# Gate projections and the first heads' keys and queries by Strassen's seven products, in a first stage of their own

## The chip, the core and the metric

The kernel runs on one core of one Trainium2 chip. The metric is the device time of one execution in microseconds (us). The engines are named as the profile names them: PE is the tensor engine with its products and transposes, DVE the vector engine, ACT the scalar engine, POOL the engine that masks and that issues the accumulating transfers, SP the engine that issues the other transfers.

## What is computed

One decoder layer for 1024 tokens with 1024 channels. All data is float32.

```
h = rmsnorm(x, norm1_g) * (1 + sc1) + sh1
p = h @ w_in                                   # 1024 x 7168
xr, yr, q, k, v, ga, gb = split(p, 7)          # components 0 to 6, 8 heads of 128 each
y_a = rg_lru(causal_dwconv(xr)) * gelu(yr)
y_b = stick_breaking_attention(rmsnorm(q), rmsnorm(k), v)
mix = sigmoid(ga) * y_a + sigmoid(gb) * y_b
x = x + gt1 * (mix @ w_out)
h2 = rmsnorm(x, norm2_g) * (1 + sc2) + sh2
g, v = split(causal_dwconv(h2 @ ffn_up), 2)
x = x + gt2 * ((gelu(g) * v) @ ffn_down)
```

sc, sh and gt are slices of c @ ada_w + ada_b, the modulation, computed on DVE as dot products. Stick-breaking attention weighs key j for query i by beta_ij times the product of (1 − beta) over the keys between them; DVE forms that product with a scan.

## The kernel before

Every factor of a product is split into a high part, rounded to the format PE takes, and a low part, the rest. A product then is three PE passes: high by high, high by low, low by high. The high part is an ACT copy or activation; the low part is a DVE subtraction (lo_of). So a projection of one component and head, 1024 inputs to 128 outputs for 1024 tokens, is 8 blocks x 3 passes x 2 halves of the tokens = 48 products of 128x512 (gemm, L150).

The program's stages, in order:

- The first stage is ordered by hand (manual_schedule). It loads the eight token tiles xr, squares all of them on ACT (L218), takes one reciprocal root on DVE, norms the tiles (L231 on DVE, L229 on ACT), and then goes through units of a channel block j and a half of the tokens hf: four transposes on PE (px, L238), two activations that modulate (hh, the high part, and hn), the low part on DVE (hl). The projections of k, q and the second branch's gate of head 0 (components 3, 2, 6, listed in FIRST) follow unit by unit in six banks of PSUM. The modulation of a channel block is two dot products over 1024 elements on DVE (L135) with two small operations (scale_shift); it stands between the units, two channel blocks ahead.
- Then eight attention heads. Here a scheduler orders the instructions by priority; with high_priority code goes ahead of what was written before it. For head h: qk(h) projects keys and queries, takes statistics st on PE, a root on DVE, sends the root through DRAM (rkd, rb), and makes the keys kh, kl. values(h), for two heads at a time, projects v. attention(h) goes through four groups of two query blocks: scores z (L418 to L420), two sigmoids on ACT, masks on POOL, the scan on DVE (L436), a multiply on DVE (L440), transposes tp on PE (L444), high and low parts ah, al, and the weighted sum py (L457). Each group also does one dot product of the modulation for later stages. gate_b(h) projects the gate of the second branch (component 6), and its sigmoid stays in the tiles sg until the head's output is multiplied.
- After head 7, early_ga projects the first branch's gate (component 5) of heads 0 to 3 into tiles of their own. The scheduler spreads these products over attention(7).
- The RG-LRU stage (lru_head, gate(1, h), lru_tail) goes over eight heads and projects the gate of component 5 for heads 4 to 7. Then out_block, the output projection.
- The FFN's up-projection runs by Strassen's seven products: the two rows of outputs (columns f and f + 24), the two halves of the inputs and the two halves of the tokens are a 2x2 by 2x2 block product, done with 7 half-size products instead of 8. A half-size product is 4 blocks x 3 passes = 12 products of 128x512. Sums of weight blocks are made by transfers that accumulate in SBUF (POOL issues them, L764); sums of h are made on DVE. For the first six columns, products 1 and 2 run early, with the first half of the tokens, and their results go to DRAM (yed).

Each engine executes its instructions in program order; an instruction that waits holds back all behind it on its engine.

## Time and profile before

| | |
|---|---|
| median of 3 runs | 1669.05 us (1667.24 to 1669.6) |
| profiled execution | 1669.8 us, of which the span of the profile is 1668.1 |
| mean granted clock of PE | 0.999 |
| 0 to 71 us | first stage |
| 71 to 645 us | attention heads |
| 645 to 852 us | RG-LRU stage |
| 852 to 983 us | output projection and the FFN's start |
| 983 to 1402 us | FFN, up |
| 1402 to 1668 us | FFN, down |

The limits of the stages are read from the timeline to about 10 us; they overlap. In the views, a row of groups reads: line, engine, operation, output <- inputs, shapes, count | busy time in all, mean ns of one | idle time before them and what ended it. A row of the timeline reads: start, duration, engine, line, operation, count, and in brackets how long the engine had waited and for what.

### The profile page before, as it was taken

To read this page: it belongs to the slowest core of one execution; us is meant where nothing else is said; L and a number is where in the kernel's file an instruction comes from. 1 tells how busy PE (TensorE), PEld (TensorE's weight loads), DVE (VectorE), ACT (ScalarE), POOL (GpSimd) and SP (SyncE) were. 2 spreads that over 40 slices of the span, in tenths; PEclk is the share of its full clock that TensorE was granted. 3 is DMA by queue.
4 is the path that set the end of the run, shared out by engine and by line. 5 is a ranking of instruction groups with operands and counts; after the bars stand their busy time and mean duration, and the time that the engine had idled before them with its cause. 6 is when DMAs were issued, how large, how long until landed. Compare 5 with 4: busy or idle time off the path is not lost.

```text
span 1668.1 us, 22133 instructions
## 1 busy us (share of the span) xinstructions
PE 1631.1 (98%) x8170; PEld 1370.6 (82%) x8170; DVE 1072.2 (64%) x1740; ACT 809.5 (49%) x1359; POOL 167.0 (10%) x340
## 2 busy tenths in 40 slices
PE   3999999999999999999999999999999999999999
PEld 2888898898898887888888878888888887888887
DVE  6676856857957734766575588866666667425372
ACT  5655544644635526775564554454554446423100
POOL 0011111110100100000000022111111110001110
PEclk9999999999999999999999999999999999999999
DMA  9122222322222232221142487655666557514232
GB/s 356 52 90 85 81 77 78 99 77 77 83 89 83 70 126 70 73 85 53 43 157 95 145 205 194 150 129 131 144 135 153 132 115 215 166 61 152 67 122 101
DMA packets 91916, 192.49 MB, mean 115 GB/s; under 512 B 9808, under 2 KB 19232, under 8 KB 91808
## 3 DMA queue, kind: packets, MB, share of 16 engines
q1 hardware_dynamic: 77984, 165.91, 29.7%
q0 software_dynamic: 13824, 25.17, 9.3%
q8 instruction: 64, 1.05, 0.3%
q14 instruction: 44, 0.36, 0.1%
HBM read 162.69 MB, written 28.35 MB: 115 GB/s over the span
## 4 chain that ended last, share of the span: by engine, by line
PE 89%; DMA 3%; ACT 3%; DVE 2%; issue 2%; POOL 0%; SPq 0%; ACTq 0%; POOLq 0%; DVEq 0%
PE acc L150 28%; PE ad L1068 16%; PE bx L812 13%; PE by L812 7%; PE accv L391 6%; PE ao L660 5%; PE py L457 3%; PE bz L812 3%; PE tp L444 2%; PE e L812 1%; PE z L419 1%; PE z L420 1%; PE z L418 1%; PE st L335 1%; DMA R<-in_ffn_up_dram 1%
## 5 line engine op out<-in xcount | busy, mean ns | idle before, releaser
L764 POOL DMA_DIRECT2D R<-in_ffn_up_dram x72 | 62.3, 897 | 575.5 <-DMA R<-in_ffn_up_dram 426.4
L1082 DVE TENSOR_TENSOR sum<-ad,sum 128x1024 f32<-128x1024 f32 (+1 forms) x26 | 29.4, 1140 | 84.8 <-PE ad L1068 83.1
L902 ACT COPY yv<-bx 128x512 f32<-128x512 f32 x36 | 21.1, 587 | 117.4 <-PE bx L812 117.3
L423 ACT ACTIVATE stk<-z,rkq 128x128 f32<-128x128 f32 (+3 forms) x96 | 57.1, 595 | 38.4 <-PE z L420 28.6
L60 DVE TENSOR_TENSOR ul<-Q,uh 128x512 fp32r<-128x512 f32 x42 | 28.9, 689 | 63.9 <-ACT uh L717 63.9
L428 POOL TENSOR_SCALAR_AFFINE_SELECT stk<-stk 128x128 f32<-128x128 f32 x64 | 23.7, 370 | 438.9 <-ACT stk L423 422.1
L436 DVE TENSOR_TENSOR_SCAN stk<-stk 128x128 f32<-128x128 f32 (+1 forms) x64 | 53.8, 840 | 15.7 <-POOL stk L432 10.2
L836 DVE SCALAR_TENSOR_TENSOR c<-yg,par,c 128x1023 f32<-128x1023 f32 (+1 forms) x48 | 61.5, 1280 | 2.9 <-ACT c L834 2.3
L60 DVE TENSOR_TENSOR ul<-R,uh 128x512 fp32r<-128x512 f32 x72 | 48.0, 688 | 21.0 <-ACT uh L717 21.0
L836 DVE SCALAR_TENSOR_TENSOR c<-yv,par,c 128x1023 f32<-128x1023 f32 (+1 forms) x48 | 61.3, 1276 | 0.0
L717 ACT CAST uh<-R 128x512 fp32r<-128x512 f32 x72 | 42.8, 619 | 36.5 <-DMA R<-in_ffn_up_dram 34.3
L135 DVE SCALAR_TENSOR_TENSOR ada<-ada,cb 128x1024 f32<-128x1024 f32 x48 | 58.4, 1227 | 1.9 <-DMA ada<-in_ada_t_dram 1.9
L440 DVE TENSOR_TENSOR beta<-beta,stk 128x128 f32<-128x128 f32 (+3 forms) x96 | 53.9, 561 | 8.2 <-POOL stk L428 0.3
L60 DVE TENSOR_TENSOR al<-tp,ah 128x128 fp32r<-128x128 f32 (+3 forms) x96 | 51.7, 549 | 11.0 <-ACT ah L446 10.8
L446 ACT CAST ah<-tp 128x128 fp32r<-128x128 f32 (+3 forms) x96 | 45.3, 489 | 27.3 <-PE tp L444 19.1
L424 ACT ACTIVATE beta<-z,rkq 128x128 f32<-128x128 f32 (+3 forms) x96 | 56.9, 593 | 0.0
L444 PE MATMUL tp<-ident,beta 128*128 128x128 f32 x288 | 46.1, 274 | 0.0
L457 PE MATMUL py<-al,vh 128*128 128x256 f32 (+1 forms) x160 | 45.5, 284 | 0.0
L457 PE MATMUL py<-ah,vl 128*128 128x256 f32 (+1 forms) x160 | 44.9, 281 | 0.0
L457 PE MATMUL py<-ah,vh 128*128 128x256 f32 (+1 forms) x160 | 44.2, 276 | 0.0
L548 ACT ACT_TABLE_LOAD x32 | 41.1, 1283 | 3.7 <-PE pg_ba L578 3.2
L436 DVE TENSOR_TENSOR_SCAN stk<-stk,stk 128x512 f32<-128x512 f32 x32 | 40.9, 1278 | 1.7 <-ACT stk L423 1.2
(522 smaller groups left out, 5453.8 us busy)
## 6 DMA issues: line engine op xcount, KB each, us to landing
ada<-in_ada_t_dram SPq DMA_DIRECT2D x48, 512.0 KB, 3.8
R<-in_ffn_up_dram POOLq DMA_DIRECT2D x72, 256.0 KB, 5.4
td<-c SPq DMA_DIRECT2D x24, 512.0 KB, 3.8
dn<-td SPq DMA_DIRECT2D x48, 256.0 KB, 7.4
dn<-in_ffn_down_dram SPq DMA_DIRECT2D x48, 256.0 KB, 3.6
R<-in_ffn_up_dram SPq DMA_DIRECT2D x24, 256.0 KB, 4.3
Q<-in_ffn_up_dram SPq DMA_DIRECT2D x24, 256.0 KB, 5.4
Q<-in_ffn_up_dram POOLq DMA_DIRECT2D x24, 256.0 KB, 4.0
```

Of the source, the lines that this page charges most:

```text
L60: return tt(out=out_, in0=full, in1=hi_.bitcast(F32), op=ALU.subtract)
L135: stt(out=t, in0=t, scalar=1.0, in1=cb, op0=ALU.mult, op1=ALU.mult, accum_out=mod[:, n:n + 1])
L150: mm(acc[hf], w[:, k % 4], r[k][hf], start=(k == 0 and i == 0), stop=(k == NB - 1 and i == 2))
L391: mm(acc[:, t * 2 * P:(t + 1) * 2 * P], r[k][hf][:, ts_], w[:, k % 2], start=(k == 0 and i == 0 and t == 0), stop=(k == NB - 1 and i == 2 ...
L436: nc.vector.tensor_tensor_scan(out=rev, data0=rev, data1=rev, initial=1.0 if last else right, op0=ALU.mult, op1=ALU.bypass)
L444: nc.tensor.transpose(tp[:, t * P:(t + 1) * P], beta[:, t * P:(t + 1) * P], ident)
L457: mm(py[:, e0 * P:2 * P], vv[:, kb, d0:d0 + P], aa[kb // 4][:, kb % 4, e0:2], start=(kb == 0 and i == 0), stop=(kb == nkb - 1 and i == 2))
L660: mm(halves(acc, nf), m[k][hf][:, ts_], w[nf], start=(k == 0 and i == 0), stop=(k == NB - 1 and i == 2))
L764: nc.gpsimd.dma_start(blk(raw[f, key]), piece(f, row, half), accum_op=ALU.add)
L812: mm(bank, w[a][:, ks], Bm[n][b][k], start=(first and k == 0 and i == 0), stop=(last and k == 3 and i == 2), skip_group_check=True)
L836: stt(out=cs[f, i][:, d:], in0=y[:, :S - d], scalar=col("fw", (2 - d) * 48 + j), in1=cs[f, i][:, d:], op0=ALU.mult, op1=ALU.add)
L1068: mm(halves(acc, nf), dparts[f, hf][a][:, ts_], dparts[f, 2 + nf][w], start=(first and i == 0), stop=(last and i == 2))
```

## The change

The FFN's seven-product functions become a class, Seven, with the same order of products for the FFN. A second instance, gates, runs over eight pairs of projections, PAIRS: the second branch's gates of heads 0 to 7 two by two, the first branch's gates of heads 4 and 5, 6 and 7, and the keys with the queries of heads 0 and 1. They run in a new first stage, ordered by hand:

- Four token tiles are loaded, squared and normed first. For the first half of the tokens, all eight channel blocks are transposed and modulated (channels, rest), and products 1 and 2 of the pairs run on them, block by block (early, by the list after); their banks go to DRAM (yed).
- The tiles of the second half are squared between the channels and normed by norm(1, ()), written after channels(7). Then second_half(i) takes channel blocks i and 4 + i together: transposes, activations, the sums t3, t2s, b12 on DVE, and splits of the factors of products 7 and 3; keep splits those of 6, 5, 4. Products 6, 7, 5, 3, 4 follow pair by pair (begin, up).
- The gates' sigmoids go to DRAM, gbd for component 6 and gad for component 5; the keys and queries of heads 0 and 1 stay in SBUF (first_kq). One sum, b12, takes the place in SBUF of the second half's first four blocks; these come back from DRAM (b12d) during the last pair. The weights of the first two heads' values are loaded and split there too (first_w).

In the attention heads, gate_b and the projections of k and q of heads 0 and 1 are gone; sg is loaded from gbd. The first branch's gates of heads 0 to 3 (gate_a) are written behind attention(1), (3), (5) and (7), with their sigmoids sent to gad; the RG-LRU stage loads all eight from there. The tiles m1 of the heads are opened after the first stage instead of before it.

The diff, cut to its core (the members of Seven that are left out are the FFN's functions as they were, with self ahead of the names; load and x1 to x4 load, add and split the weights of a pair):

```diff
-BUFS = {"raw": 2, "wh": 4, "wl": 4, "pre": 4, "beta": 3, "sg": 4}
-WHOLE = (5, 7)
+RAWS = {"R": 3, "Q": 2, "a": 1, "d": 2}
...
-        size = max(n, P) if pool is m1 else n
+        size = P if p < P else n
...
+    class Seven:
...
+        def parts_of(self, f, n, key, tiles=None):
+            h_, l_ = tiles or self.part_tiles(f, n)
+            split(self.raw[f, key], h_, l_)
+            self.ups[f, n] = h_, l_
...
+        def add(self, f, key, row, half):
+            nc.gpsimd.dma_start(blk(self.raw[f, key]), self.piece(f, row, half), accum_op=ALU.add)
+
+
+        def x1(self, f):
+            self.parts_of(f, 5, "R")
+            self.add(f, "R", 0, 0)
...
+        def product(self, bank, f, n, first, last, ks=range(4)):
+            w = self.ups[f, n] if ks[-1] < 3 else self.ups.pop((f, n))
+            for k in ks:
+                cols_ = slice(k * P, (k + 1) * P)
+                for i, (a, b) in enumerate(((0, 0), (0, 1), (1, 0))):
+                    mm(bank, w[a][:, cols_], self.Bm[n][b][k], start=(first and k == 0 and i == 0),
+                       stop=(last and k == 3 and i == 2), skip_group_check=True)
...
+        def begin(self, f):
+
+            if f >= self.nf:
+                return
+            bx = self.bank(f"bx{f}")
+            if f < self.n_early:
+                yg = self.begun_early.pop(f)
+                self.product(bx, f, 6, True, False)
+                if f in self.stay:
+                    yv = btile(f"yv{f}")
+                else:
+                    yv = self.F.tile([P, S], F32, tag="es", name=f"yv{f}", bufs=self.es_bufs)
+                tt(out=halves(yv, 0), in0=bx, in1=halves(yg, 1), op=ALU.add)
...
+                order = (7, 5, 0, 3, 4)
+                if f + 1 < early_n:
+                    todo = {1: [(x2, f + 1)], 2: [(x4, f)], 3: [(a22, f)] + [(x1, f + 2)] * (f + 2 < early_n), 4: [],
+                            5: [(x3, f + 1)]}
...
+    gbd = dram.tile([HEADS, P, S], F32, name="gbd")
+    gad = dram.tile([HEADS, P, S], F32, name="gad")
...
+    def first_bank(name, count=[-1]):
...
+    def gate_steps(f):
+        def finish(row):
+            comp, h = PAIRS[f][row]
+            y = gates.ys[f][row]
+            if f in gates.stay:
+                first_kq[comp, h] = y
+                return
+            act(y, y, AF.Sigmoid)
+            nc.sync.dma_start((gbd if comp == 6 else gad)[h], y)
...
+    PAIRS = ([((6, h), (6, h + 1)) for h in range(0, HEADS, 2)] + [((5, h), (5, h + 1)) for h in range(4, HEADS, 2)]
+             + [((3, h), (2, h)) for h in range(2)])
...
+    gates = Seven(NP, NP, pair_piece, yed, first_bank, None, gate_steps)
+    gates.stay = (NP - 2, NP - 1)
...
+    turns1 = ([(f, 1) for f in range(5)] + [(f, 2) for f in range(4)]
+              + [(5, 1), (4, 2), (6, 1), (5, 2), (7, 1), (6, 2), (7, 2)])
+    raw_of = "WWRRRQQddWWdWdWd"
...
+        def rest(j):
+            n, i = (1, j) if j < 4 else (2, j - 4)
+            lo_of(gates.Bm[n][1][i], (t2s, t4s)[n - 1][i], gates.Bm[n][0][i])
...
+        def early(f, n, ks=range(4)):
+            if n == 1 and ks[0] == 0:
+                gates.banks_of[f] = first_bank(f"e{f}")
+            bank = gates.banks_of[f]
+            gates.product(bank, f, n, n == 1, n == 2, ks)
+            if ks[-1] == 3:
+                es = etile(f"es{f}_{n}")
+                nc.scalar.copy(es, bank)
+                nc.sync.dma_start(halves(yed[f], 2 - n), es)
...
+        def second_half(i):
+
+            modulated(transposed(f"px{i}_1", 1, i), i, b12[i])
+            nc.sync.dma_start(b12d[i], b12[i])
+            modulated(transposed(f"px{4 + i}_1", 1, 4 + i), 4 + i, b22[i])
+            t3[i] = etile(f"t3_{i}")
+            tt(out=t3[i], in0=b12[i], in1=b22[i], op=ALU.subtract)
+
+            tt(out=t2s[i], in0=t3[i], in1=t2s[i], op=ALU.subtract)
+            stt(out=b12[i], in0=t2s[i], scalar=-1.0, in1=b22[i], op0=ALU.mult, op1=ALU.subtract)
+            split(t3[i], gates.Bm[7][0][i], gates.Bm[7][1][i])
+            keep(3, i)
...
+        after = [[(0, 1, (0,)), (1, 1, (0,))],
+                 [(0, 1, (1,)), (1, 1, (1,)), (2, 1, (0, 1)), (3, 1, (0, 1))],
+                 [(f, 1, (2,)) for f in range(4)], [(f, 1, (3,)) for f in range(4)],
+                 [(0, 2, (0,)), (1, 2, (0,)), (4, 1, range(4)), (2, 2, (0,))],
+                 [(0, 2, (1,)), (1, 2, (1,)), (2, 2, (1,)), (3, 2, (0, 1))],
+                 [(f, 2, (2,)) for f in range(4)] + [(5, 1, range(4))], [(f, 2, (3,)) for f in range(4)]]
...
+        load_mod(0)
+        for t in range(4):
+            load_x(t)
+        weights(2)
+        load_mod(1)
+        weights(2)
+        load_mod(2)
         scale_shift(0, *ada.pop(0))
...
+        norm(0, (1, 3))
+        channels(0)
+        parts(0)
+        rest(0)
+        parts(1)
         scale_shift(1, *ada.pop(1))
-        weights(6, "beta", "sg")
-        for n, (j, hf) in enumerate(units):
-            if n + 2 < len(units):
-                channels(n + 2)
-                rest(n + 2)
-            for comp, _ in FIRST[n < 2:]:
-                gemm(first_acc[comp], first_w[comp], hi, lo, (hf,), (j,))
-            if n % 2 == 0 and n // 2 + 2 < NB:
-                scale_shift(n // 2 + 2, *ada.pop(n // 2 + 2))
-            elif n // 2 + 6 < NB:
-                ada[n // 2 + 6] = load_modulation(n // 2 + 6)
+        channels(1)
...
+        for j in range(NB):
+            for do in fetch[j]:
+                do()
+            if j + 2 < NB:
+                scale_shift(j + 2, *ada.pop(j + 2))
+            if j + 1 < NB:
+                rest(j + 1)
+            for q in splits[j]:
+                parts(q)
+            for f, n, ks in after[j]:
+                early(f, n, ks)
+            if j + 2 < NB:
+                channels(j + 2)
+            for t in {2: (4,), 3: (5,), 4: (6,), 5: (7,)}.get(j, ()):
+                squares(t)
+            if j == 5:
+                norm(1, ())
...
+        for s_ in range(6):
+            early(*turns1[10 + s_])
+            if s_ < 4:
+                second_half(s_)
+                parts(12 + s_)
...
+        gates.begin(0)
+        keep(5, 2)
+        keep(5, 3)
+        gates.up(0, {1: [lambda: keep(4, 0)], 2: [lambda: keep(4, 1), lambda: keep(4, 2)], 3: [lambda: keep(4, 3)]})
+        for f in range(1, NP - 1):
+            gates.up(f)
...
+        if (comp, h) in first_kq:
+            with tc.high_priority(offset=AHEAD):
+                for hf in range(2):
+                    evac(hf, halves(first_kq[comp, h], hf))
+            return
...
-        parts = wsplit(w_in, 4 * NB + h, 2, f"wv{h}")
+        parts = wsplit(w_in, 4 * NB + h, 2, f"wv{h}") if h else first_w
...
+    def gate_a(h):
+
+        def evac_g(hf, acc):
+            g = m1.tile([P, H2], F32, tag="ga", name=f"ga{h}_{hf}", bufs=2)
+            act(g, acc, AF.Sigmoid)
+            nc.sync.dma_start(halves(gad[h], hf), g)
+
+        proj(5, h, evac_g)
...
     for h in range(HEADS):
         y = m1.tile([P, S], F32, tag="y", name=f"yb{h}", bufs=2)
+        sg = m1.tile([P, S], F32, tag="sg", name=f"sg{h}", bufs=2)
+        nc.sync.dma_start(sg, gbd[h])
         qkh = qk(h)
         if h % 2 == 0:
-            sg = gate_b(h)
             vt = values(h)
-            attention(h, y, *qkh, vt)
-        else:
-            attention(h, y, *qkh, vt)
-            if h in (3, 7):
-                gate_row(h // 7)
-            sg = gate_b(h)
+        attention(h, y, *qkh, vt)
+        if h in (3, 7):
+            gate_row(h // 7)
+        for g in {1: [0], 3: [1], 5: [2], 7: [3]}.get(h, ()):
+            gate_a(g)
         for hf in range(2):
-            tt(out=halves(y, hf), in0=halves(y, hf), in1=sg[hf], op=ALU.mult)
+            tt(out=halves(y, hf), in0=halves(y, hf), in1=halves(sg, hf), op=ALU.mult)
         nc.sync.dma_start(ybd[h], y)
-
-    early_ga = []
-    for h in range(4):
-        early_ga.append(btile(f"ga{h}"))
-        proj(5, h, lambda hf, acc: act(halves(early_ga[-1], hf), acc, AF.Sigmoid))
...
-            ga = gate(5, h, AF.Sigmoid) if h >= len(early_ga) else [halves(early_ga[h], hf) for hf in range(2)]
+            ga = [t2("gate5", h, hf) for hf in range(2)]
+            for hf in range(2):
+                nc.sync.dma_start(ga[hf], halves(gad[h], hf))
```

The first place is DVE in the first stage. Before, the low part of a unit (hl and channel, half) and the modulation of a channel block (ada, s1, mod) take turns:

```order
L60 TENSOR_TENSOR hl1_0_266<-hn1_0_263,hh1_0_262 128x512
L135 SCALAR_TENSOR_TENSOR ada10_137,mod_81<-ada10_137,cb_88 128x1024
L135 SCALAR_TENSOR_TENSOR ada2_138,mod_81<-ada2_138,cb_88 128x1024
L172 SCALAR_TENSOR_TENSOR s1_90<-mod_81,ab1_97,par_79 128x1
L174 TENSOR_TENSOR mod_81<-mod_81,par_79 128x1
L60 TENSOR_TENSOR hl1_1_287<-hn1_1_284,hh1_1_283 128x512
L60 TENSOR_TENSOR hl2_0_308<-hn2_0_305,hh2_0_304 128x512
L135 SCALAR_TENSOR_TENSOR ada11_141,mod_81<-ada11_141,cb_88 128x1024
L135 SCALAR_TENSOR_TENSOR ada3_142,mod_81<-ada3_142,cb_88 128x1024
L172 SCALAR_TENSOR_TENSOR s1_90<-mod_81,ab1_97,par_79 128x1
L174 TENSOR_TENSOR mod_81<-mod_81,par_79 128x1
L60 TENSOR_TENSOR hl2_1_332<-hn2_1_329,hh2_1_328 128x512
```

After, b2l, ul are low parts of the first half's channels 4 to 7 and of weights, r1_1 is the second half's root, xr4 to xr7 its tiles, t3 the first sum of the second half:

```order
L101 SCALAR_TENSOR_TENSOR r1_1t_509<-r1_1r_508 128x4
L102 TENSOR_TENSOR r1_1t_509<-r1_1t_509,r1_1m_507 128x4
L103 SCALAR_TENSOR_TENSOR r1_1r_508<-r1_1t_509,r1_1r_508 128x4
L494 TENSOR_SCALAR xr4_120<-xr4_120,r1_1r_508 128x1024
L494 TENSOR_SCALAR xr5_121<-xr5_121,r1_1r_508 128x1024
L494 TENSOR_SCALAR xr6_122<-xr6_122,r1_1r_508 128x1024
L494 TENSOR_SCALAR xr7_123<-xr7_123,r1_1r_508 128x1024
L59 TENSOR_TENSOR b2l3_497<-n4_3_155,b2h3_496 128x512
L59 TENSOR_TENSOR ul4_2_594<-e2_4_420,uh4_2_593 128x512
L59 TENSOR_TENSOR ul6_1_598<-e1_6_467,uh6_1_597 128x512
```

The second norm now stands between channel 6's low part and b2l3, that of channel 7, and the second half's sums follow directly.

The second place is PE in attention(7). Before, z7 are scores, and acc5_1_1 is a bank of the first branch's gate of head 1:

```order
L419 MATMUL z7_4_0_6131<-kl7_5981,qh7_5768 128x512
L420 MATMUL z7_4_0_6131<-kh7_5980,ql7_5769 128x512
L150 MATMUL acc5_1_1_6502<-hl0_1_229,w5_1h0_6466 128x512
L150 MATMUL acc5_1_1_6502<-hh0_1_225,w5_1l0_6467 128x512
L150 MATMUL acc5_1_1_6502<-hh1_1_283,w5_1h0_6466 128x512
L150 MATMUL acc5_1_1_6502<-hl1_1_287,w5_1h0_6466 128x512
L150 MATMUL acc5_1_1_6502<-hh1_1_283,w5_1l0_6467 128x512
L150 MATMUL acc5_1_1_6502<-hh2_1_328,w5_1h0_6466 128x512
L418 MATMUL z7_5_1_6149<-kh7_5980,qh7_5768 128x256
L419 MATMUL z7_5_1_6149<-kl7_5981,qh7_5768 128x256
L420 MATMUL z7_5_1_6149<-kh7_5980,ql7_5769 128x256
L150 MATMUL acc5_1_1_6502<-hl2_1_332,w5_1h0_6466 128x512
```

After, at the same place:

```order
L779 MATMUL z7_3_0_6874<-kh7_6786,qh7_6574 128x512
L780 MATMUL z7_3_0_6874<-kl7_6787,qh7_6574 128x512
L781 MATMUL z7_3_0_6874<-kh7_6786,ql7_6575 128x512
L805 MATMUL tp7_0_0_6815<-ident_67,beta7_0_0_6804 128x128
L805 MATMUL tp7_1_0_6834<-ident_67,beta7_1_0_6823 128x128 x2
L779 MATMUL z7_4_1_6918<-kh7_6786,qh7_6574 128x128
L780 MATMUL z7_4_1_6918<-kl7_6787,qh7_6574 128x128
L781 MATMUL z7_4_1_6918<-kh7_6786,ql7_6575 128x128
L779 MATMUL z7_4_0_6937<-kh7_6786,qh7_6574 128x512
L780 MATMUL z7_4_0_6937<-kl7_6787,qh7_6574 128x512
L781 MATMUL z7_4_0_6937<-kh7_6786,ql7_6575 128x512
L805 MATMUL tp7_2_0_6868<-ident_67,beta7_2_0_6857 128x128 x3
```

Between the scores (z7) and the transposes (tp7) of head 7 no projection is left.

The third place is PE ahead of head 7's first scores, after the change; py6_3 is the last weighted sum of head 6, rt7 the transposed roots of head 7, acc5_3_1 the last gate of component 5:

```order
L818 MATMUL py6_3_6541<-ah6_3_1_6455,vh6_6029 128x128
L818 MATMUL py6_3_6541<-al6_3_1_6457,vh6_6029 128x128
L818 MATMUL py6_3_6541<-ah6_3_1_6455,vl6_6030 128x128
L146 MATMUL acc5_3_1_7175<-b3h2_738,w5_3l1_7144 128x512
L146 MATMUL acc5_3_1_7175<-b3h3_787,w5_3h1_7143 128x512
L722 MATMUL rt7_6780<-ident_67,r7r_6765 128x16
L146 MATMUL acc5_3_1_7175<-b3l3_788,w5_3h1_7143 128x512
L146 MATMUL acc5_3_1_7175<-b3h3_787,w5_3l1_7144 128x512
L779 MATMUL z7_0_0_6800<-kh7_6786,qh7_6574 128x128
L779 MATMUL z7_1_0_6819<-kh7_6786,qh7_6574 128x256
L780 MATMUL z7_0_0_6800<-kl7_6787,qh7_6574 128x128
L781 MATMUL z7_0_0_6800<-kh7_6786,ql7_6575 128x128
```

The last gate's products, written behind attention(7), stand ahead of its first score; before, the first scores of head 7 had the products of acc5_0 and acc5_1 behind them.

609 lines of the change are left out of this document (304 added, 305 removed).

## Prediction

> **What bounds the kernel now.** The head of the page comes first, then the chain that ended last, then the busy times by stretch.
>
> ```profile
> span 1668.1 us, 22133 instructions
> PE 1631.1 (98%) x8170; PEld 1370.6 (82%) x8170; DVE 1072.2 (64%) x1740; ACT 809.5 (49%) x1359; POOL 167.0 (10%) x340
> PE 89%; DMA 3%; ACT 3%; DVE 2%; issue 2%; POOL 0%; SPq 0%; ACTq 0%; POOLq 0%; DVEq 0%
> ```
>
> The tensor engine is busy for all but 37 us, so the time is its work plus what it loses. The stretches tell where it loses, and how near the vector engine is to taking over:
>
> ```profile
> core 0: us, PE busy (x) PEld busy (x) DVE busy (x) ACT busy (x) POOL busy (x), PEclk, DMA share, GB/s
> 0.00:29.00 29.00, 3.54 (x10) 1.73 (x10) 14.92 (x56) 16.95 (x28) 1.52 (x11) 1.00 0.96 361
> 29.00:65.00 36.00, 36.00 (x173) 29.48 (x174) 29.72 (x62) 21.82 (x33) 0.00 (x0) 1.00 0.49 167
> ...
> 226.00:355.00 129.00, 129.00 (x810) 113.01 (x810) 92.15 (x169) 65.37 (x133) 16.74 (x56) 1.00 0.25 82
> ...
> 645.00:852.00 207.00, 204.78 (x893) 168.07 (x892) 135.39 (x204) 142.58 (x212) 0.00 (x0) 0.99 0.20 63
> ...
> 983.00:1036.00 53.00, 51.85 (x226) 41.62 (x225) 46.71 (x62) 22.62 (x31) 12.58 (x15) 1.00 0.77 180
> ```
>
> 226:355 is two attention heads with their projections: PE never rests, DVE has 92 of 129 us. The margin is there because projections fill PE while the attention chain runs. 983:1036 is the FFN's seven-product code on its early columns: PE 51.85 of 53 us with DMA at 0.77, so that code keeps PE fed once under way. The first stage loses at its front:
>
> ```profile
> PE px L238 <- DVE xr L231: 24.4, 4, 23.9
> PE acc L150 <- DVE hl L60: 0.9, 1, 0.9
> ```
>
> **1. Products removed.** Two long runs of products and one run of transposes give the pitch of each kind:
>
> ```profile
> 207.15 18.76 PE accv L391 x156
> ...
> 1044.50 5.44 PE by L812 x24
> ```
>
> ```profile
> 30.34 0.63 PE L150 MATMUL acc<-hl,w_0h 128*128 128x512 f32 x1
> 30.77 0.63 PE L150 MATMUL acc<-hh,w_0l 128*128 128x512 f32 x1
> ...
> 61.86 0.60 PE L238 MATMUL px<-ident,xr 128*128 128x128 f32 x4
> 62.21 0.48 PE L150 MATMUL acc<-hh,w_0h 128*128 128x512 f32 x1
> ...
> 70.74 0.39 PE L150 MATMUL acc<-hh,w_0l 128*128 128x512 f32 x1
> ```
>
> A 128x512 product costs 5.44/24 = 0.227 us, a 256-wide one 18.76/156 = 0.120, four transposes 62.21 − 61.86 = 0.35. The sixteen projections that become eight pairs took 16 × 48 = 768 products; seven products of half size per pair are 8 × 7 × 12 = 672. 96 fewer × 0.227 = **−21.8 us**, and this is all that the change can win on PE's work.
>
> **2. First stage.** Before, its last product is at 70.74 + 0.23 = 70.97. The work in it is 144 × 0.227 + 64 × 0.0875 = 38.3, so PE lost 32.7. After, the first eight channels of the first half need four squares, not eight:
>
> ```profile
> 15.21 0.19 ACT L218 ACTIVATION_READ_ACCUMULATOR junk<-xr 128x1 f32 x1
> ```
>
> ```profile
> 20.54 0.17 DVE L97 TENSOR_SCALAR r1m<-ss 128x8 f32<-128x8 f32 x1 [7.77 <-ACT junk L218]
> 22.97 4.07 DVE L231 TENSOR_SCALAR xr<-xr,r1r 128x1024 f32<-128x1024 f32 x6
> 26.95 1.29 DVE L60 TENSOR_TENSOR w_0l<-w_0r,w_0h 128x512 fp32r<-128x512 f32 x2
> ...
> 45.17 1.22 DVE L135 SCALAR_TENSOR_TENSOR ada<-ada,cb 128x1024 f32<-128x1024 f32 x1
> ...
> 47.66 0.69 DVE L60 TENSOR_TENSOR hl<-hn,hh 128x512 fp32r<-128x512 f32 x1
> ```
>
> The fourth square ends at 15.40 and the eighth at 20.5, so the start moves 5 us ahead. A reciprocal root costs 22.97 − 20.54 = 2.43, a row tile's norm 4.07/6 = 0.68, a low part 1.29/2, pitch about 0.62, and one channel's modulation 47.66 − 45.17 = 2.49. But DVE now does the first half of all eight channels with all seven modulations before the second norm: 15.40 + 2.43 + 2 × 0.68 = 19.2, then 17 low parts × 0.62 + 7 × 2.49 = 28.0, the second root and four norms 5.1, and channel 7's low part, in hand order behind that norm: 33.7 us of work. In 29:65, the same kind of queue, DVE was busy 29.72 of 36 us, 83%. At that rate the last low part lands at 19.2 + 33.7/0.83 = 59.8. Up to there PE has only 108 products and 32 transposes, 27.3 us. The second half is paced by DVE too: per pair of channels seven operations of 0.62 and one hand-over of about 0.7 (an estimate; the 0.9 us wait above is the nearest row) are 5.1 us, against 12 products and 8 transposes, 3.4 us, on PE. PE needs 12 + 12 products and 8 transposes, then ACT and DVE a step each, before the first of four such pairs: about 67.3; plus 20.4 and the last 12 products gives 90.9 where 192 × 0.227 + 64 × 0.0875 = 49.1 us are done. Lost 41.8 against 32.7: **+9**. Bounds: the 5 us earlier start with nothing lost behind it gives −5; a DVE only 75% filled, in the queue and in the pairs, gives +15. After it, pairs go as in 983:1036, where DVE's 46.71 of 53 us leaves little; I take no further loss (0 to +5). The added transfers (gates, early sums, b12 out and back) have room: 0.25 of DMA in 226:355, 0.77 in 983:1036; only 0:29 is full at 0.96, and there four row tiles fewer are fetched ahead of the first norm.
>
> **3. Attention heads.** The gate projections and k, q of two heads leave this part, so PE has less to do beside each chain. DVE's own work per head comes from these groups, over eight heads (48 dots, four in each head):
>
> ```profile
> L436 DVE TENSOR_TENSOR_SCAN stk<-stk 128x128 f32<-128x128 f32 (+1 forms) x64 | 53.8, 840 | 15.7 <-POOL stk L432 10.2
> ...
> L135 DVE SCALAR_TENSOR_TENSOR ada<-ada,cb 128x1024 f32<-128x1024 f32 x48 | 58.4, 1227 | 1.9 <-DMA ada<-in_ada_t_dram 1.9
> L440 DVE TENSOR_TENSOR beta<-beta,stk 128x128 f32<-128x128 f32 (+3 forms) x96 | 53.9, 561 | 8.2 <-POOL stk L428 0.3
> L60 DVE TENSOR_TENSOR al<-tp,ah 128x128 fp32r<-128x128 f32 (+3 forms) x96 | 51.7, 549 | 11.0 <-ACT ah L446 10.8
> ...
> L436 DVE TENSOR_TENSOR_SCAN stk<-stk,stk 128x512 f32<-128x512 f32 x32 | 40.9, 1278 | 1.7 <-ACT stk L423 1.2
> ```
>
> (53.8 + 40.9)/8 + 53.9/8 + 51.7/8 + 4 × 1.23 = 30 us. PE's own (scores, transposes, weighted sums) is 14.6 by its counts and the pitches above; projections must fill the rest. I counted, in the new order, each engine's instructions from one head's first score to the next one's, at the same prices.
> - Heads 0 and 1: DVE 24 scans 23.7, 23 multiplies 12.9, 20 low parts of weights 11.0, 24 other low parts 14.9, 7 dots 8.1, two roots 4.9: 75.5. PE 137 projection products 31.1, 96 of the values 11.5, and own work: 67.6. DVE is late by **+8** (3 if its queue runs ahead from the first stage, 15 at 90% filled).
> - Head 3: 41 on DVE, 36.7 on PE (44 products, 96 of the values): **+4** (1 to 9). Heads 2, 4, 5, 6 have PE ahead by 3 to 20 us; nothing.
> - Head 7's scores wait for its keys:
>
> ```profile
> 79.81 0.28 DVE L97 TENSOR_SCALAR r0m<-st 16x128 f32<-16x128 f32 x1 [0.18 <-PE st L335]
> ...
> 90.76 1.33 DVE L60 TENSOR_TENSOR kl<-kg,kh 128x512 fp32r<-128x512 f32 x2
> ```
>
> From the statistics to the keys' low part, 92.1 − 79.8 = 12.3 us. The new order has 23 products and 24 weighted sums, 8.1 us, between. **+4** (2 to 6); all of head 7 is queued behind these scores.
> - Head 7 itself has **no projection left**: the last gate's products (acc5_3) all stand ahead of its scores, and behind it comes the next stage, in order. PE has 14.6 us of work while DVE has 29.2 by its counts. Add a lead of 1.8 (score, sigmoid, select), about 3 of hand-overs, and a tail of 24 weighted sums at 0.12 with the last cast, 3.4; with overlap, about 38 long: **+23** (19.8 if only DVE's 30 and the tail count; 30 if every block's hand-over shows).
> - Waits for the values' buffers and at the stage's end: **+2** (0 to 6).
>
> The pitch between 30.34 and 30.77 is 0.43 where 0.227 is usual, 3 us after PE's long wait, and it is back by the later rows, though the window's granted clock reads 1.00: after a wait PE runs at half rate for a while. The Trainium skill's "TensorE: Matmul & The Clock Gate", section "Part 1: The HAM clock gate", says that an idle window of about 3.4 us puts the array at half rate until it has been busy as long; the pitch agrees. By that rule a wait in head 7 of that length would halve PE behind it; without it nothing.
>
> **4. RG-LRU stage and FFN.** In 645:852 PE is at 204.78 of 207 with ACT at 142.58, over heads with and without a gate projection; the second kind is what is left, with sigmoids fewer and loads from DRAM at a DMA share of 0.20 to hide in: 0 (to +3). The FFN's order is unchanged.
>
> **Sum** on the profiled execution's 1669.8 us (span 1668.1 and 1.7 around it; 0.75 above the median of 1669.05, so nothing to correct): −21.8 + 9 + 8 + 4 + 4 + 23 + 2 = +28.2: **1698 us**.
>
> **Rivals.**
> - *Not slower.* PE's count rules: the earlier start pays for the second half (0, not +9), heads 0 to 3 and the keys cost nothing because DVE's queue runs ahead of PE from the first stage on, and head 7 costs 19.8. 1669.8 − 21.8 + 19.8 = 1668. It decides where the losses together stay below 21.8 us. For it: PE was never idle in 226:355. Against it: there 140 products filled every head, and head 7 now has none. Chance 0.18 with its neighbours up to 1672.
> - *DVE binds more.* Queues of hand-overs leave DVE 85% filled in heads 0, 1 and 3 (+13 and +6 more than DVE's sum against PE's) and head 7 costs 30: about 1715. For it: the 83% in 29:65. Against: 226:355 shows long DVE runs without a wait. Chance 0.2.
> - *Half of it.* First stage 0 and heads 0 to 3 half, head 7 at 20: about 1682. Chance 0.1.
> - *It doesn't do what it says*: the projections still plain, or products doubled. The order shows 672; 0.02.
>
> - *PE at half rate through head 7*: at 0.43/0.227 its lead (0.8 us of scores and transposes) and its tail (2.9 us of weighted sums) grow by 0.9 of themselves, 3.3 us, and a few transposes between blocks 1.5: 1703, inside the forecast's spread and 0.1 of the chance there. The clock gate page of the Trainium skill would expect this one.
>
> **Numbers.** Forecast 0.5 (1688 to 1708). To leave out at most 2 in 10, the range spans the half case and the DVE case, from 1672 to 1720. A measurement of this kernel tells 0.2% (3.3 us) from no change. Faster 0.14 and same 0.06 come from the first rival and the last; slower 0.8 is the rest.
>
> **What would show it.** The last product of the early kind near 80 to 90 us, with waits of PE on low parts of n4 and splits of n2, n12 (step 2); if it is below 75, step 2 is wrong. No wait of PE from there to the end of the gates' pairs. In head 7, a stretch of about 38 us with PE below half busy, its waits on DVE's al and the scan's multiply (step 3); if acc5_3 fills it, or if it is under 30 us, the sum is wrong by 10 or more. PE busy down by about 20 us in all. It would be wrong altogether if the gates' pairs wait on their accumulating transfers, 3 us a pair making +25, or if DVE kept up in every head.

## The result, and the profile after

The changed kernel takes 1730.79 us (median of 4 runs, 1727.69 to 1731.92) against 1668.36 before (4 runs): a ratio of 1.0371, with a 95% interval of 1.0353 to 1.0389, 62 us slower. The forecast was 1698 us and a range up to 1720: the direction held, and the size was under half of what came.

The head of the page of the changed kernel: span, busy time of each engine, and the chain that ended last by engine.

```profile
span 1728.8 us, 22399 instructions
PE 1645.4 (95%) x8074; PEld 1370.5 (79%) x8074; DVE 1127.1 (65%) x1848; ACT 833.9 (48%) x1402; POOL 207.8 (12%) x372
PE 71%; DVE 9%; DMA 7%; issue 6%; ACT 6%; POOL 1%; SPq 0%; ACTq 0%; POOLq 0%; DVEq 0%
```

PE executes 96 products fewer (x8074 for x8170), yet its busy time rises by 14 us, and the chain of waits lies outside PE for 29% of the span instead of 11%. Busy time misleads here: a product that runs at half clock counts as longer work (records of 0.63 us instead of 0.39), and one that runs alone counts its whole record of 0.39 us or more, where in a run of products each adds 0.227. So the table below counts work, not busy time: the trace's number of products in each stretch, each at the pitch of its kind in undisturbed stretches (0.227, 0.120 and 0.0875 us as in the forecast, 0.176 for 384 columns, 0.06 for the statistics). What a stretch lasts beyond that is lost.

| stretch | before: us, lost | after: us, lost | loss more |
|---|---|---|---|
| first stage, to the first gate pair | 71.0, 32.7 | 100.5, 51.4 | +18.7 |
| gate pairs | | 124.5, 13.3 | +13.3 |
| to head 0's first score | 25.6, 0.5 | 25.6, 0.7 | +0.2 |
| heads 0 to 2 | 188.4, 6.2 | 170.0, 16.6 | +10.4 |
| heads 3 to 6 | 258.7, 8.0 | 236.4, 19.5 | +11.5 |
| head 7 | 53.3, 1.3 | 35.4, 19.0 | +17.7 |
| RG-LRU | 247.8, 6.5 | 199.9, 6.6 | +0.1 |
| output projection | 44.4, 0.9 | 64.6, 13.4 | +12.5 |
| FFN, to the end | 774.9, 7.2 | 768.0, 5.4 | -1.8 |

The sum of the last column is +82.6; the counted work fell by 21.9; together 60.7 us, which is the difference of the two spans. Some of the stretches of the changed kernel in the windows view: the first stage, the gate pairs, head 1, head 2, heads 3 to 6, head 7 and the output projection. A row has the length, then busy time and number of instructions of PE, PEld, DVE, ACT and POOL, then the granted clock of PE, the DMA share and GB/s:

```profile
0.00:100.50 100.50, 64.18 (x256) 48.46 (x257) 64.78 (x158) 54.47 (x92) 8.63 (x16) 0.97 0.81 268
100.50:225.00 124.50, 117.31 (x500) 94.07 (x499) 61.50 (x96) 42.50 (x68) 21.10 (x25) 0.97 0.73 186
...
290.20:328.50 38.30, 37.57 (x274) 34.33 (x272) 36.77 (x74) 23.00 (x50) 8.49 (x28) 1.00 0.34 111
328.50:420.60 92.10, 87.14 (x511) 74.49 (x512) 58.38 (x106) 42.35 (x84) 11.35 (x32) 0.98 0.28 93
420.60:657.00 236.40, 228.91 (x1473) 202.77 (x1471) 177.18 (x329) 123.38 (x250) 35.62 (x111) 0.99 0.29 94
657.00:692.50 35.50, 25.27 (x133) 20.11 (x133) 30.65 (x53) 19.42 (x40) 9.72 (x26) 0.86 0.46 161
...
892.30:957.00 64.70, 57.96 (x228) 45.39 (x228) 50.62 (x102) 37.35 (x59) 0.00 (x0) 0.92 0.42 155
```

Head 7 and the output projection in the kernel before:

```profile
543.70:597.00 53.30, 53.30 (x291) 45.70 (x290) 34.30 (x57) 25.83 (x53) 7.42 (x25) 1.00 0.30 104
...
844.70:889.20 44.50, 43.95 (x194) 35.94 (x193) 32.83 (x79) 25.62 (x39) 0.00 (x0) 1.00 0.52 190
```

In the changed kernel each stretch that lost over 10 us more has a granted clock below 1.00, between 0.86 and 0.99. The waits behind these losses are of four kinds. First, the first stage, as the timelines of DVE and PE show it (the bracket has the idle time before the instruction and what ended it):

```profile
77.28 0.69 DVE L530 SCALAR_TENSOR_TENSOR n<-n,n 128x512 f32<-128x512 f32 x1 [2.24 <-DMA b12d<-n]
...
91.07 0.69 DVE L530 SCALAR_TENSOR_TENSOR n<-n,n 128x512 f32<-128x512 f32 x1 [3.67 <-DMA b12d<-n]
```

```profile
79.83 0.72 PE L259 MATMUL e<-b2h,ul 128*128 128x512 f32 x1 [3.04 <-DVE ul L59]
80.35 0.63 PE L259 MATMUL e<-b2h,uh 128*128 128x512 f32 x1
...
93.62 0.79 PE L259 MATMUL e<-b2h,ul 128*128 128x512 f32 x1 [4.46 <-DVE ul L59]
```

`second_half` stores b12[i] to DRAM and then overwrites it in place (L530). DVE waits until the store has read the tile; the weights' low parts ul are queued behind it, and PE waits for those. Behind each of the two waits PE runs at half rate: its next products start 0.43 us apart (from 80.35 to 82.91 and from 94.21 to 96.77), where 0.227 is usual. Second, POOL's queue in the gate pairs, and the waits that it makes:

```profile
145.33 0.86 POOL L206 DMA_DIRECT2D Q<-in_w_in_dram  x1 [7.84 <-DMA Q<-in_w_in_dram]
145.88 2.16 POOL L206 DMA_DIRECT2D R<-in_w_in_dram  x2
```

```profile
ACT uh L156 <- DMA R<-in_w_in_dram: 69.3, 7, 13.2
...
POOL Q L206 <- DMA Q<-in_w_in_dram: 39.9, 5, 8.8
...
PE bx L259 <- ACT uh L156: 6.6, 3, 3.2
```

POOL issues the accumulating transfers in order. The one for Q waits for Q's plain load to land, 8 us in each of five pairs (39.9 in all), and the sums for R that stand behind it go out only then, at once. ACT waits 69.3 us in all for R, and PE 6.6 us for the high parts that ACT makes from it. Third and fourth, heads with uneven filling work, and the output projection, come with the experiments.

### The profile page after: what moved, and what is told of

Same layout as the page of the kernel before. It is cut to its first block, busy times and chain, and to the rows that moved or that the text cites. A ratio compares the mean times of both kernels' runs of the same rounds, so it can differ in the third digit from the quotient of the medians.

```text
span 1728.8 us, 22399 instructions
## 1 busy us (share of the span) xinstructions
PE 1645.4 (95%) x8074; PEld 1370.5 (79%) x8074; DVE 1127.1 (65%) x1848; ACT 833.9 (48%) x1402; POOL 207.8 (12%) x372
## 4 chain that ended last, share of the span: by engine, by line
PE 71%; DVE 9%; DMA 7%; issue 6%; ACT 6%; POOL 1%; SPq 0%; ACTq 0%; POOLq 0%; DVEq 0%
PE ad L1212 15%; PE bx L259 15%; PE acc L146 13%; PE by L259 8%; PE accv L752 4%; PE ao L1016 4%; PE bz L259 3%; PE e L259 3%; DMA R<-in_w_in_dram 2%; PE py L818 2%; DMA Q<-in_w_in_dram 2%; DVE stk L797 1%; ACT L902 1%; PE tp L805 1%; DVE ada L131 1%
## 5 line engine op out<-in xcount | busy, mean ns | idle before, releaser
L156 ACT CAST uh<-R 128x512 fp32r<-128x512 f32 x96 | 57.5, 617 | 100.1 <-DMA R<-in_w_in_dram 69.3
L59 DVE TENSOR_TENSOR ul<-R,uh 128x512 fp32r<-128x512 f32 x96 | 64.5, 688 | 49.6 <-ACT uh L156 49.5
L59 DVE TENSOR_TENSOR ul<-Q,uh 128x512 fp32r<-128x512 f32 x50 | 34.4, 688 | 64.7 <-ACT uh L156 64.7
L789 POOL TENSOR_SCALAR_AFFINE_SELECT stk<-stk 128x128 f32<-128x128 f32 x64 | 30.2, 471 | 294.2 <-ACT stk L784 284.7
L259 PE MATMUL bx<-b6h,uh 128*128 128x512 f32 x128 | 51.3, 401 | 6.6 <-ACT uh L156 6.6
L259 PE MATMUL bx<-b6h,ul 128*128 128x512 f32 x128 | 51.5, 402 | 0.0
L259 PE MATMUL bx<-b3h,uh 128*128 128x512 f32 x128 | 50.3, 393 | 1.2 <-ACT yv L327 0.7
L259 PE MATMUL bx<-b6l,uh 128*128 128x512 f32 x128 | 51.1, 399 | 0.0
```

The costliest lines, as they stand in the source:

```text
L59: return tt(out=out_, in0=full, in1=hi_.bitcast(F32), op=ALU.subtract)
L259: mm(bank, w[a][:, cols_], self.Bm[n][b][k], start=(first and k == 0 and i == 0), stop=(last and k == 3 and i == 2), skip_group_check=True)
```

## The experiments

All are compared with the kernel before, run on the same chip; its median there lay between 1668.2 and 1669.9 us, so 2 us between two rows tell little. "Lost" is counted as in the table. bx0 is the first bank of the first gate pair, and its time is the start of that pair.

| run | us | ratio to before, 95% interval |
|---|---|---|
| changed kernel | 1730.8 | 1.0371 (1.0353 to 1.0389) |
| e1_b12_late | 1727.0 | 1.0351 (1.0334 to 1.0368) |
| e2_q_late | 1717.8 | 1.0290 (1.0269 to 1.0311) |
| e3_fill_123 | 1736.7 | 1.0404 (1.0388 to 1.0419) |
| e4_tail7_f012 | 1732.5 | 1.0379 (1.0362 to 1.0397) |
| e5_v2buf | 1708.6 | 1.0238 (1.0221 to 1.0255) |
| e6_b12_norm | 1725.9 | 1.0344 (1.0329 to 1.0360) |
| e7_warm | 1739.9 | 1.0424 (1.0406 to 1.0441) |
| e8_all | 1684.8 | 1.0094 (1.0078 to 1.0109) |
| e9_first | 1726.6 | 1.0343 (1.0328 to 1.0359) |
| e10_warm_st | 1733.9 | 1.0383 (1.0367 to 1.0398) |
| e11_all2 | 1683.0 | 1.0082 (1.0065 to 1.0099) |
| e12_hold | 1682.0 | 1.0080 (1.0063 to 1.0097) |
| e13_double | 1725.5 | 1.0344 (1.0327 to 1.0362) |
| e14_best | 1683.5 | 1.0089 (1.0074 to 1.0104) |

### e1: the sum that overwrites b12, later

```diff
-            stt(out=b12[i], in0=t2s[i], scalar=-1.0, in1=b22[i], op0=ALU.mult, op1=ALU.subtract)
...
-                5: [lambda: t4(0), lambda: t4(1), lambda: t4(2), lambda: t4(3), lambda: keep(5, 0), lambda: keep(5, 1)]}
+                5: [lambda: t4(0), lambda: t4(1), lambda: t4(2), lambda: t4(3)] + [lambda i=i: sum12(i) for i in range(4)]
+                + [lambda: keep(5, 0), lambda: keep(5, 1)]}
```

> One edit against the changed kernel (1730.8 us): in second_half the sum that overwrites b12[i] is taken out and all four are done later, after t4. Theory A, a store in the way: in the changed kernel DVE stood 2.2 and 3.7 us behind the store of b12 to b12d before that sum, PE then waited 3.0 and 4.5 us for low parts queued behind it, and ran two windows of 3.4 us at half clock after them. Then these waits and both half-clock windows go, the first gate pair (bx0, at 100.5 us) starts at 89 to 92 us, and the time falls by 8 to 11 us, to about 1721. Rival B, DVE and ACT pace the second half by their own work: the wait comes back as another one, bx0 moves by less than 3 us, the time falls by less than 3.

The waits of DVE on the store are gone and the first pair starts at 92.5 us instead of 100.5, just above the 89 to 92 of theory A. Not all of these 8 us is the store's. Ahead of the edited code e1 already ran 1.2 us earlier (the second root starts at 57.2 us, 58.4 in the changed kernel). From the first sum t3 to bx0 it took 20.1 us instead of 26.9, 6.8 less; the two waits on the store had been 5.9 of that. In the six profiles that leave the first stage as it was (the changed kernel, e3, e4, e5, e7, e10) bx0 stands at 100.5 to 102.2 us, in the eight with this sum late (e1, e6, e8, e9, e11 to e14) at 92.5 to 96.7. The windows view of e1, to its first pair:

```profile
0.00:92.50 92.50, 60.56 (x257) 45.09 (x258) 62.48 (x155) 54.28 (x92) 7.61 (x15) 0.98 0.85 289
```

The time fell by 3.8 us only, and the two intervals overlap. What came back: the pairs took 126.1 us (124.5), and head 7, unchanged in order, 38.0 (35.4), with more of it at half clock. So the store's cost is shown at its place, about 6 us; in the whole time no more than 3.8 came back, and that is not clear of noise.

### e2: Q's accumulating load behind R's

```diff
-                self.add(f, "Q", 1, 0)
...
-                todo[4] = todo[4] + [(self.load_d, f + 1)]
+                todo[4] = todo[4] + [(self.load_d, f + 1), (self.add_q, f + 2)]
```

> One edit against the changed kernel (1730.8 us), in the gate pairs only: the accumulating load of Q is issued two slots later than its plain load, behind those of R on POOL's queue. Theory A, POOL's queue is held by Q: POOL waits 7.5 to 8.8 us per pair for Q's plain load to land before it issues Q's sum, and two sums for R stand behind; ACT then waits 69 us in all for R and PE waits 6.6 us for weights, with two half-clock windows. Then POOL's wait for Q goes, ACT's wait for R at least halves, the pairs take 112 to 117 us instead of 124.5, and the time falls by 7 to 12 us, to about 1721. Rival B, the transfers themselves are the limit (DMA share 0.75, 5.5 us a sum, five in a chain for each pair): the pairs take 122 us or more, and the time stays within 3 us.

The waits and the window of the pairs in e2:

```profile
ACT uh L156 <- DMA R<-in_w_in_dram: 53.1, 8, 9.6
```

```profile
99.30:213.40 114.10, 113.01 (x500) 92.21 (x499) 61.61 (x96) 43.15 (x68) 21.13 (x25) 1.00 0.78 203
```

The pairs take 114.1 us and lose 3.0 (13.3); the granted clock is 1.00, and the time falls by 13.0 us, of which 10.4 are in the pairs. Theory A, a little beyond its span: POOL's waits for Q fell from 39.9 to 4.5 us, and PE's for the high parts from 6.6 to 0.5. ACT's wait for R did not halve as expected, 53.1 us are left; but an engine that is early may wait, and PE no longer does. The transfers have room: the DMA share rose from 0.73 to 0.78.

### e3 and e4: where the plain gates stand

```diff
-        for g in {1: [0], 3: [1], 5: [2], 7: [3]}.get(h, ()):
+        for g in {3: [0], 7: [1, 2, 3]}.get(h, ()):
```

> Against the changed kernel (1730.8 us) only the places at which the first branch's plain gates are written: head 0's behind attention(3), those of heads 1, 2 and 3 behind attention(7). The work is the same; in the order, 60 products then stand between the first score and the last weighted sum of head 7 (none before), 78 in head 0 (137), 25 in head 5 (60). Theory A, head 7 is bare: its 35.4 us, 19.0 of them lost, with 13.6 us of products put in lose 4 to 8 us, the wait of 2.5 us for its keys goes, heads 0 and 5 lose up to 5 us more; the time falls by 8 to 15 us, to about 1719. Rival B, the products are only moved and the loss moves with them, to heads 0, 3 and 5: within 3 us.

Rival B, and worse than its 3 us: 5.9 us slower. Head 7, with 60 products in it, took 44.0 us (35.4) and lost 13.9 us (19.0), but head 0 lost 12.0 (1.8), and all eight together 65.2 (55.1). Head 0 of e3 in the windows view:

```profile
251.90:290.20 38.30, 32.11 (x185) 25.87 (x184) 36.71 (x74) 25.62 (x54) 13.01 (x28) 0.91 0.28 89
```

DVE is busy 36.71 of 38.30 us: a head that gives up its filling work is bound by DVE, as the forecast had it.

```diff
-             + [((5, h), (5, h + 1)) for h in range(4, HEADS, 2)]
+             + [((5, h), (5, h + 1)) for h in (3, 5)]
...
-            ga = [t2("gate5", h, hf) for hf in range(2)]
+            if h == 7:
+                ga = gate(5, h, AF.Sigmoid)
+            else:
+                ga = [t2("gate5", h, hf) for hf in range(2)]
```

> Against the third kernel of this set (e3_fill_123): the pairs of component 5 are heads 3 and 4, 5 and 6; head 7's gate is a plain projection in the RG-LRU stage, as in the kernel before, and those of heads 0 to 2 are written behind attention(7). The number of products is the same; head 7's attention has 60 of them in both, head 3's has 25 instead of 60. Theory A, the end of the RG-LRU stage is uncovered: in the changed kernel the output projection lost 13.4 us with three waits of about 2 and three half-clock windows, since nothing stood beside head 7's recurrence; with 48 products there, it loses 1 to 4, and head 3 loses up to 4 more: 5 to 11 us less than e3. Rival B, the output projection waits for its own weights or for the norm: within 3 us of e3.

The time is 4.2 us below e3, just under theory A's span, and the two intervals overlap, but the place is clear. The output projection in the changed kernel (what PE waited for), and in e4 (its window):

```profile
PE ao L1016 <- ACT woh L882: 2.2, 2, 2.0
PE ao L1016 <- DVE og L1020: 2.0, 1, 2.0
PE ao L1016 <- DVE xc L920: 1.9, 1, 1.9
```

```profile
906.10:955.40 49.30, 46.93 (x204) 37.83 (x203) 36.87 (x82) 31.52 (x48) 0.00 (x0) 1.00 0.51 182
```

With 48 products beside head 7's recurrence the projection loses 3.3 us (11.7 in e3, 13.4 in the changed kernel), RG-LRU 7.2 (5.5 in e3), and the clock stays at 1.00.

### e5: two buffers for the values

```diff
-        vh = m1.tile([P, NB, 2 * P], F32R, tag="vh", name=f"vh{h}")
-        vl = m1.tile([P, NB, 2 * P], F32R, tag="vl", name=f"vl{h}")
+        vh = m1.tile([P, NB, 2 * P], F32R, tag="vh", name=f"vh{h}", bufs=2)
+        vl = m1.tile([P, NB, 2 * P], F32R, tag="vl", name=f"vl{h}", bufs=2)
```

> Against the changed kernel (1730.8 us): the tiles vh and vl of the values have two buffers instead of one (sg one instead of two, to make room). The work is the same. In the order, all four banks of the values of heads 2 and 3 then stand in head 1 (two and two before, in heads 1 and 2), and 166 small products in place of 219 in head 2. Theory A, the values' single buffer bunches the filling work: the values' first two banks held both PSUM buffers named acc until the odd head was over, so PE had nothing else there, and DVE's backlog came out as 11.8 us lost at the start of head 2 and 6.4 in head 5 (a wait of 2.8 for vl). Then heads 1 to 6 lose 10 to 18 us less than the 34.3 of the changed kernel, and the time falls by 8 to 18 us. Rival B, heads 1 to 3 and 5 are bound by DVE's own work (36.8 of 38.3 us busy in head 1), wherever the filling work stands: less than 4 us.

The time fell by 22.2 us, more than theory A's 18, with the same products. What PE waited for longest in heads 0 to 6, in the changed kernel and then in e5:

```profile
PE accv L752 <- DVE vl L59: 4.0, 3, 2.8
PE z L779 <- ACT beta L785: 2.8, 5, 1.1
```

```profile
PE z L779 <- ACT kh L734: 2.6, 1, 2.6
PE py L818 <- DVE al L59: 0.4, 1, 0.4
```

Heads 1 and 2 of e5:

```profile
291.10:346.20 55.10, 54.72 (x423) 51.93 (x422) 49.23 (x93) 30.72 (x63) 9.92 (x32) 1.00 0.31 97
346.20:406.40 60.20, 60.20 (x344) 51.13 (x343) 45.10 (x83) 33.32 (x67) 8.24 (x28) 1.00 0.37 122
```

Head 1 has grown from 38.3 to 55.1 us and head 2 shrunk from 92.1 to 60.2: the values of the next two heads moved from the second to the first, and PE is full in both. Heads 1 to 6 lose 15.3 us instead of 34.3. This is the largest single gain of the trials, and the buffer is not in the change at all: the kernel before has the same single one, and lost 2 us a head with it. That its other filling work covered the rest fits this; two buffers in the kernel before were not tried.

### e6, e9, e13: what else holds the first stage

```diff
+            if j == 6:
+                norm(1, ())
...
-            if j == 5:
-                norm(1, ())
```

> Against e1_b12_late (1727.0 us, bx0 at 92.5): norm(1, ()), the second half's root and four norms, is written behind rest(7) instead of ahead of it. Theory A: the low part of channel 7 then comes about 5 us sooner, PE's wait of 3.2 us for it and the wait of 1.2 behind it go, and the second half's start moves by less; bx0 comes at 88 to 90 us, the time falls by 2 to 5 us. Rival B, the second half's norm is what counts, and it is only 0.6 us later: bx0 within 1 us, the time within 2 us.

bx0 at 94.2 us, 1.7 later than in e1, which is no more than the spread of bx0 between unchanged first stages; the time 1.1 us less: rival B. PE's wait for channel 7's low part went, and one of 5.2 us for a high part of the weights came instead.

```diff
+        scale_shift(1, *ada.pop(1))
         channels(0)
...
-        scale_shift(1, *ada.pop(1))
```

> Against e1_b12_late (1727.0 us, bx0 at 92.5): in the first stage alone, the modulation of channel 1 stands right behind the first norm instead of behind the weights' low parts, each channel's low part stands ahead of the next modulation, and the late sum of b12[i] is done one pair later instead of all four at the end. Theory A, DVE's order at the front: DVE stood idle 3.3 us behind the first norm with the modulation of channel 1 still to do, ACT waited 4.0 us for that and PE ran 18.6 to 36 us with 34 products; then these waits go, bx0 comes at 86 to 89 us, the time falls by 3 to 6 us. Rival B, the loads or ACT set the front: bx0 within 2 us.

Neither theory: bx0 at 96.2 us, 3.7 later than in e1, and the time the same (1726.6 us). The front is quicker (PE executes 62 instructions between 18.6 and 36 us, 39 in e1), but PE then waits 3.6 us for ACT's copies of early sums, which stand behind the modulation on ACT, and 4.9 for channel 7.

```diff
                 nc.sync.dma_start(halves(yed[f], 2 - n), es)
+                nc.sync.dma_start(halves(td[f], 2 - n), es)
```

> Against e1_b12_late (1727.0 us, bx0 at 92.5): each of the sixteen early sums is stored twice, the second time to a part of DRAM (td) that nothing reads before the FFN writes it; 4.2 MB more, no other instruction. Theory A, transfers bind the first stage: at the 400 GB/s of its busiest stretch these are 10 us of transfers; ACT's waits for the stores of early sums (3.4 us in e1) at least double, bx0 comes at 96 to 103 us and the time rises by 4 to 11 us. Rival B, the transfers have room and the engines' hand-overs bind: bx0 within 1.5 us, the time within 3.

The time did not move (1725.5 us), and ACT's wait for the stores went from 3.4 to 4.1 us and did not double. But bx0 came 3.1 us later, more than rival B allows and less than theory A's 3.5 to 10.5: the transfers, at a DMA share of 0.99 to 1.06 from 36 us on, are at most a part of the bind. What holds the first stage at a loss of 43 us, 10 more than before, is left open; a place gained there has come back as another wait in each trial.

### e7 and e10: products that only keep PE busy in head 7

```diff
+                    if h == 7:
+                        with tc.issue_after(last_tp.ins):
+                            for _ in range(4):
+                                mm(warm, hi[0][0][:, :P], hi[1][0], start=True, stop=True)
```

> Against the changed kernel (1730.8 us): behind each of head 7's twelve groups of transposes stand four products whose result is never read, 48 x 0.227 = 10.9 us of PE work more. Theory A, the half clock costs time in a bare head: head 7 took 35.4, 38.0 and 38.0 us in the three profiles of this order, with 10.0, 20.5 and 20.5 us at half clock; the added products keep PE at full clock, the half-clock windows there go from 3 to 6 down to at most 1, and head 7 takes 33 to 37 us in spite of them; the time is the same or up to 3 us less. Rival B, PE's waits in head 7 only follow DVE's and ACT's chain, and the clock is of no account: the added products stand ahead of scores and weighted sums that are ready, and head 7 takes 38 to 44 us; the time rises by 3 to 8 us.

9.1 us slower, but it doesn't tell: the tile warm took one of two PSUM buffers, and the last gate's 48 products moved behind head 7's first scores.

> The test of e7_warm again without its side effect (there the added tile took one of two PSUM buffers and pushed the last gate's products behind head 7's first scores): the 48 unread products now write the buffer st, and all other instructions stand in the changed kernel's order (1730.8 us). In five profiles of that order of head 7 it took 35.4 us with 10.0 at half clock and 36.5 to 38.0 with 16 to 20.5. Theory A, the half clock costs 2 to 4 us there: head 7 takes 33 to 36 us with at most one half-clock window, although 10.9 us of PE work were added; the time is the same or up to 3 us less. Rival B, the clock does not matter to a chain of DVE and ACT, or the added products delay it: head 7 takes 38 us or more.

Head 7 in e1 (the changed order) and in e10:

```profile
651.90:689.90 38.00, 29.21 (x133) 23.79 (x133) 30.77 (x53) 19.19 (x40) 10.85 (x26) 0.73 0.42 150
```

```profile
658.50:696.20 37.70, 34.47 (x181) 28.55 (x181) 30.97 (x53) 19.44 (x40) 9.24 (x26) 0.86 0.43 152
```

48 products more and head 7 takes 37.7 us, inside the 35.4 to 38.0 that it takes without them; the time, 1733.9 us, is within noise of the changed kernel. The number lies between the two theories. So PE's work is not what sets head 7; what is left is DVE's 30.97 us and the hand-overs. But the added products did not keep the clock up either (0.86), so what half clock costs there is left open.

### e8, e11, e12, e14: together

e8 joins the edits of e1, e2, e4, e5 and e6; heads 0 to 2's gates stand behind attention(0), (7) and (7), with the last spread over head 7. e11 has e9's first stage instead, e12 holds a gate's products back for the wait on head 7's keys, e14 is e12 with e1's first stage.

> All that helped, together, against the changed kernel (1730.8 us): the sum of b12 late (e1), Q's sum late (e2), the second norm behind channel 7 (e6), the values' tiles double (e5), head 7's gate of component 5 plain in the RG-LRU stage (e4); heads 0 to 2's gates behind attention(0), (7) and (7), the last of them in four pieces of 12 products held back behind transposes of head 7. By the parts: first stage -8 and -3, pairs -10, output projection -8, heads -10 to -18, head 7 -5: 1678 to 1690, still slower than the kernel before (1669). Rival, the parts fill the same gaps: 1695 or more. If it is under 1669, the heads bind less than I think.

> As e8_all (1684.8 us), but with e9's first stage and the second norm in its old place (e6 gained nothing from moving it: bx0 94.2 against 92.5). By the parts: first stage -5 to -7, first pairs -2: 1675 to 1680. Rival: what the first stage gains is lost again in the pairs, which wait for their sums of weights: 1682 or more.

> As e11_all2, but the products of the gate of head 1 (component 5) are held behind the statistics of head 7's keys and queries: 44 products then stand between these and head 7's first score (22 in e11). In e8_all PE waited 3.9 us there for the keys (12.3 us of work on DVE, ACT and the way through DRAM). Theory A: that wait goes to under 1 us, head 6 loses up to 2 more, the time is 1 to 4 us less than e11. Rival B, head 6 is then short of work by as much: within 1 us of e11.

> As e12_hold (1682.0 us) but with e1's first stage (bx0 at 92.5 there, 96.7 in e12). By the parts: first stage -4: 1677 to 1680, still above the kernel before (1669). Rival: as in e8_all, where the earlier start was lost again in the pairs (116.5 us against 113): 1681 or more.

e8 gains 46 us of the 62, as expected. The three after it missed: they lie within 1.5 us of each other, e11 and e14 in their rivals' spans, and e12's 1.0 us below e11 is not clear of noise. In e12 the wait of 3.4 us for head 7's keys went, and one of 2.7 for the statistics came ahead of it; e14 started its pairs at 95.2 us instead of 96.7, and they took 115.9 us instead of 113.7. None beats the kernel before; the lowest, e12, is 0.8% slower (0.6% to 1.0%).

## Why the prediction was wrong

- **Products removed, -21.8**: right; the counted work fell by 21.9.
- **First stage, +9**: measured +18.7. The first pair starts at 100.5 us where the forecast had 90.9 (its terms, as they stand, add to 90.4). Two steps failed. One is "at that rate", DVE 83% filled. The changed kernel between the first norm and the last low part:

```profile
19.20:64.10 44.90, 35.98 (x140) 27.05 (x139) 33.68 (x76) 24.33 (x41) 2.02 (x2) 1.00 0.80 278
```

  DVE did just the 33.7 us of work that the forecast had counted, but in 44.9 us, 75% filled, the case that the forecast kept for its upper bound: the last low part landed at 64.1 instead of 59.8, 4.3 us late. Another 2.0 were lost from there to the first sum t3. The other step is the pacing "per pair of channels seven operations of 0.62 and one hand-over": I priced the seven operations and not that one of them overwrites a tile under a running store. From the first t3 to bx0 it took 26.9 us where the forecast had 23.6, and 5.9 of them are the two waits on that store. The added transfers were costed by the DMA share, as room, not as something to wait for.
- **Gate pairs, "I take no further loss (0 to +5)"**: measured +13.3, and e2 takes 10.3 of it away. The failed step is "pairs go as in 983:1036". That row told of the same code under lighter conditions: between 980 and 1060 us of the kernel before, POOL waited 13.0 us for Q and ACT 21.3 for R, and PE hardly lost by it. POOL's queue, in which Q's sum holds R's, stood in the order and I did not walk along it. The line on what would make the forecast wrong named it, at 3 us a pair, without a chance.
- **Heads 0 and 1, +8, and head 3, +4**: measured +0.8 and +2.0, but +9.6 in head 2, for which the forecast had nothing. The size came out, one head later: DVE was busy for 19.5 of the 20 us around the start of head 2 (325 to 345). The reason held only in part, as e5 takes this loss away without touching DVE's work. DVE bound a head where the values' single buffer kept filling work out of it.
- **Heads 4 to 6, nothing, and the wait for head 7's keys, +4**: measured +9.5 together. In it are a wait of 2.5 for the keys, partly the same buffer (a wait of 2.8 for vl in head 5; in e5 heads 4 and 5 lose no more than before), and two half-clock windows behind short waits.
- **Head 7, +23**: measured +17.7; 35.4 us long where 38 was forecast. The mechanism held: DVE was busy for 30.65 us of it, and the longest waits of PE were for al (2.7 and 2.0). With 48 products more it took 37.7 us in e10, and 35.7 to 36.1 in e8, e11 and e12, where they are a gate's. With the 60 of e3 it took 44.0; why these lengthened it is not shown. Small waits, +2: nothing seen beyond these.
- **RG-LRU and after, "0 (to +3)"**: RG-LRU +0.1, but the output projection +12.5. The failed step is "the second kind is what is left": the forecast looked at heads without a gate projection in the middle of the stage, where the next head covers, and not at the last one, where head 7's gate had covered the end of the recurrence. With it back (e4) the projection loses 3.3.

The first stage (9.7 us over its term), the pairs (13.3) and the output projection (12.5) make 35.5 us, and all other terms together came out 3.0 below theirs: these are the 32.5 us between the +60.7 of the spans and the +28.2 of the forecast. Of the forecast's signs, the long stretch of head 7 with waits on al came; PE's busy time went up instead of down, the last early product stood at 100.3 us and not at 80 to 90, and PE did wait in the pairs. Of the rivals, "DVE binds more" came nearest with its 1715, but by its number alone: it had the loss in heads 0, 1, 3 and 7.

## What to carry to other kernels

Work that is removed from a full engine may have been the cover of something: before a product is taken away, look at the last round of its loop, where nothing else follows. When a stage is moved or made shorter, walk along each in-order queue in it, the DMA-issuing ones too, and ask of every in-place write and accumulating load what it must wait for and who stands behind it. And where several engines share a stretch, the buffers decide where the filling work can go: one more buffer was worth 22 us here, as much as the 96 products.
